# A decoder trunk on one core: the gated convolution's input projection as block products in seven multiplications, and pairs of products taken in turns

## The chip, the cores and the metric

The kernel runs on one core of a Trainium2 chip. The core has a matrix engine (TensorE, PE in the rows; its weight loads are PEld), a vector engine (VectorE, DVE), a scalar engine (ScalarE, ACT), a general engine (GpSimd, POOL), and a queue engine for transfers (SyncE, SP). The metric is the time of one execution on the device in microseconds; the kernel before takes 2549.22 us, the median of 2549.22, 2549.35 and 2545.19.

## What is computed

A trunk of two layers over 1024 tokens of 1024 features, in fp32. Each layer is a mixer, a cross-attention into 256 memory tokens, and an MLP with squared ReLU, each with an RMS norm ahead and a residual added. The mixer of layer 0 is differential attention beside pooling; that of layer 1 is the gated convolution, which the change touches most:

```python
def odd_mixer(h, w_in, conv_w, w_out):
    S = h.shape[1]
    proj = h @ w_in                       # 1024 -> 3 * 1024
    b_gate = proj[..., :CONV_DIM]
    c_gate = proj[..., CONV_DIM:2 * CONV_DIM]
    z = c_gate * proj[..., 2 * CONV_DIM:]
    zp = jnp.pad(z, ((0, 0), (CONV_WIDTH - 1, 0), (0, 0)))
    y = zp[:, 0:S] * conv_w[0]
    for tap in range(1, CONV_WIDTH):
        y = y + zp[:, tap:tap + S] * conv_w[tap]
    return (b_gate * y) @ w_out

for l in range(DEPTH):
    h = h + mixer(rms_norm(h, norm_mix_g[l]))
    h = h + cross_attention(rms_norm(h, norm_xattn_g[l]), mem_n, xattn_wq[l], xattn_wkv[l], xattn_wo[l])
    h = h + sq_relu_mlp(rms_norm(h, norm_mlp_g[l]), mlp_w1[l], mlp_w2[l])
return rms_norm(h, final_norm_g)
```

## The kernel before

**Layout and precision.** Activations lie transposed: 128 features on the partitions, 1024 tokens along a row, eight tiles for 1024 features. A product in fp32 is made of two rounded parts per operand: `cut` writes the high part with a copy on ACT (L72) and the low part with a subtraction on DVE (L73; L75 and L76 where a gain is multiplied in). Three matmuls, high by high, high by low and low by high, make one product of a 128x128 weight tile and 512 tokens. A plain product of one output tile (`gemm`, matmuls on L201) so takes 8 x 3 x 2 = 48 matmuls of 128x512.

**Block products.** `split_gemm` (L277) makes two output tiles at once, in seven steps of 12 matmuls, 84 in all, in place of 96: the weights of the pair and the operand are taken as 2x2 blocks, and four combinations of each ("groups" 0 to 3, the last of half size) are multiplied in seven products. The operand is a `Split` (its groups made by `combine`, L259 to L262), the weights' combinations are made in `w_cut` by four additions on DVE (L149 to L153) and four cuts. The partial sums stand in three PSUM banks (`_x` and the two halves of `_yz`); after each step they are copied out by ACT or added by DVE. With `first` the first four steps are ordered so that parts that come late are used last. A set of `hooks` says what else is issued ahead of which step. Block products serve the queries (`c0q`, `c1q`: four pairs each), MLP up (`m0a`, `m1a`: 16 pairs, evacuated on L1038 and L1042) and MLP down (`m0b`, `m1b`: four chunks `c` of the hidden features by four pairs `p`, added into the residual on L1112). The groups of MLP down's operand are written to DRAM in MLP up and fetched again (`m0f`, L73 rows `m0A_g_k`). The last product of all uses another order of steps, `TAIL`.

**The convolution.** For each of eight tiles j three plain products, `cv{j}c`, `cv{j}x`, `cv{j}b`; the first two are multiplied by the norm's row factors `rbc` and by each other, run through the three taps, and multiplied by the third. MLP down of layer 0 hands over its result as eight cut tiles (L75, L76). The product with conv's output weights (`cvo`) is the `residual`, plain.

**The norm.** Squares are summed on DVE (`acc`), turned by PE (`_n`), reduced on DVE (`_ms`), raised to -1/2 on POOL (`_rcol`), and spread by PE to rows (`_b`), from which `rbc` is read. `stage1` ends with POOL, `stage2` starts with `_b`.

**Order.** The weights come in one list, `order`; SP loads them into four buffers `wr`, and `w_next` hands over a cut and makes the one after it, with two buffers each for `wh` and `wl`. A scheduler of the program's own sets the order of instructions on each engine from the order of the code, its costs and priorities; PE, ACT and DVE then run strictly in that order. 44 slots of 128x1024 hold everything else.

Of the kernel before, what the change touches and what calls it, by code (L numbers as in the profile page):

```python
# [40 lines left out]
def hybrid_trunk(ctx: ExitStack, tc: tile.TileContext, xT, memT, vecs, lams, rel, onehot, negrow, invcnt,  # L41
# [76 lines left out]
    def w_cut():  # L118
        u, g = state["unit"], state["group"]
        if u >= len(order):  # L120
            return
        shape = list(order[u][0])
# [705 lines left out]
    def residual(act, g_col, name, split=False):  # L828
# [55 lines left out]
    def cross(l, X, nrm, g_next, name):  # L884
# [20 lines left out]
        def query(p, hooks):  # L905
# [89 lines left out]
        for p, hooks in enumerate((merged(X.late, {5: [nrm.stage1]}), {1: [divide]}, {},  # L995
# [22 lines left out]
    def mlp(l, X, nrm, g_next, name):  # L1018
# [259 lines left out]
```

## Time and profile before

| | us |
|---|---|
| runs | 2549.22, 2549.35, 2545.19 |
| profiled execution | 2544.53, span 2542.8 |
| PE busy | 2498.8 (98%) |
| DVE busy | 1763.8 (69%) |
| ACT busy | 1073.4 (42%) |
| POOL busy | 25.7 (1%) |

The page is of the profiled execution, whose own time goes with its span. A row of the chain of waits gives the start, the length and the work; a row of PE's waits the engine and tile waited for, the total, the number and the longest; a row of the timeline the start, the length and the instruction, with the idle time before it and what ended it. Rows of the windows give the busy time of PE, PEld, DVE, ACT and POOL in a stretch, then the granted clock, and the share and rate of the transfers. Matmuls overlap in their records: the distance between starts is their pace.

### The profile page before, as it was taken

The page shows a single profiled execution, that of the slowest core. Times are in us where ns is not written, and L with a number is a line of the kernel's source. Part 1 is how long each engine was busy: PE and PEld are TensorE (multiplying, and loading weights), DVE is VectorE, ACT ScalarE, POOL GpSimd, SP SyncE. Part 2 cuts the span into 40 slices and gives each one's busy share as a digit, 9 for nine tenths or more (in the row PEclk, how much of TensorE's full clock was granted, in tenths as well). Part 3 has the DMA queues.
Part 4 walks back from the last instruction along what each step waited for, and adds up shares of the span by engine and source line. Part 5 has one row for each costly group of instructions (what it writes and reads, how often), then busy time and mean ns, then how long its engine had stood idle before and what let it go on. Part 6 is the DMA issues. An engine that isn't in the chain of part 4 may idle for free.

```text
span 2542.8 us, 29713 instructions
## 1 busy us (share of the span) xinstructions
PE 2498.8 (98%) x11522; PEld 2048.1 (81%) x11522; DVE 1763.8 (69%) x2339; ACT 1073.4 (42%) x1513; POOL 25.7 (1%) x24
## 2 busy tenths in 40 slices
PE   9999999999999999999999999999999999999997
PEld 6777778888878888788888888888887888778886
DVE  7777764766677777888784433576667777888876
ACT  5455664445443334443341111344544333434432
POOL 0000000000000000000000000000000000000001
PEclk9999999999999999999999999999999999999998
DMA  5111255221424346877641111422133444777752
GB/s 175 34 34 42 75 169 204 100 83 42 141 88 171 139 145 239 293 270 261 243 154 59 50 50 46 145 75 92 58 117 116 159 160 153 269 266 259 281 207 92
DMA packets 108429, 365.88 MB, mean 144 GB/s; under 512 B 12416, under 2 KB 14848, under 8 KB 108288
## 3 DMA queue, kind: packets, MB, share of 16 engines
q1 hardware_dynamic: 74880, 252.82, 29.5%
q10 hardware_dynamic: 33408, 111.16, 11.4%
q8 instruction: 91, 1.49, 0.2%
q14 instruction: 50, 0.41, 0.0%
HBM read 249.91 MB, written 114.03 MB: 143 GB/s over the span
## 4 chain that ended last, share of the span: by engine, by line
PE 89%; DVE 6%; ACT 2%; DMA 2%; issue 1%; POOL 0%; SPq 0%; ACTq 0%; DVEq 0%; POOLq 0%
PE m0a_x L277 7%; PE m1a_x L277 7%; PE m1b_x L277 7%; PE m0b_x L277 6%; PE m1a_yz L277 5%; PE m0a_yz L277 5%; PE m1b_yz L277 5%; PE m0b_yz L277 4%; PE cvo L201 3%; PE X L201 3%; PE c1o L201 3%; PE c0o L201 3%; PE kv_ps L742 3%; PE qkv L201 2%; PE c1q_x L277 2%; PE c0q_x L277 2%
## 5 line engine op out<-in xcount | busy, mean ns | idle before, releaser
L72 ACT ACTIVATE wh<-wr 128x1024 fp32r<-128x1024 f32 (+1 forms) x318 | 305.6, 961 | 777.7 <-PE m1b_yz L277 137.5
L73 DVE TENSOR_TENSOR wl<-wr,wh 128x1024 fp32r<-128x1024 f32 (+1 forms) x318 | 350.3, 1101 | 135.1 <-ACT wh L72 130.3
L72 ACT ACTIVATE wh<-wt 128x1024 fp32r<-128x1024 f32 x72 | 76.0, 1055 | 60.0 <-PE m0b_x L277 16.5
L73 DVE TENSOR_TENSOR wl<-wt,wh 128x1024 fp32r<-128x1024 f32 x72 | 87.8, 1219 | 0.9 <-ACT wh L72 0.9
L201 PE MATMUL X<-Y,wh 128*128 128x512 f32 x256 | 69.8, 389 | 0.0
L581 ACT ACTIVATE s_p<-s,s_negm 128x128 f32<-128x128 f32 (+7 forms) x64 | 47.3, 739 | 33.6 <-DVE s_negm L580 30.3
L201 PEld LDWEIGHTS X<-Y,wh 128*128 128x128 f32 x256 | 48.1, 188 | 10.0
L149 DVE TENSOR_TENSOR wt<-wr 128x512 f32<-128x512 f32 x71 | 48.8, 687 | 6.8 <-DMA wr<-in_w_dram 3.1
L150 DVE TENSOR_TENSOR wt<-wr,wt 128x512 f32<-128x512 f32 x71 | 48.9, 689 | 1.3
L152 DVE TENSOR_TENSOR wr<-wr,wr 128x512 f32<-128x512 f32 x71 | 48.7, 687 | 1.0
L153 DVE TENSOR_TENSOR wr<-wr,wt 128x512 f32<-128x512 f32 x71 | 48.6, 684 | 0.0
L1028 ACT ACTIVATE m0a_r<-m0a_r 128x1024 f32<-128x1024 f32 x32 | 33.9, 1061 | 32.0 <-DVE m0a_r L1027 31.9
L1028 ACT ACTIVATE m1a_r<-m1a_r 128x1024 f32<-128x1024 f32 x32 | 33.9, 1060 | 32.0 <-DVE m1a_r L1027 31.8
L580 DVE TENSOR_REDUCE s_negm<-s 128x1 f32<-128x128 f32 (+7 forms) x64 | 46.6, 750 | 0.2
L1042 DVE TENSOR_TENSOR m0a_r<-m0a_r,m0a_yz 128x512 f32<-128x512 f32 x32 | 21.9, 685 | 31.3 <-PE m0a_yz L277 31.1
L1042 DVE TENSOR_TENSOR m1a_r<-m1a_r,m1a_yz 128x512 f32<-128x512 f32 x32 | 21.9, 685 | 31.3 <-PE m1a_yz L277 31.1
L1038 ACT ACTIVATE m0a_r<-m0a_x 128x512 f32<-128x512 f32 x32 | 19.1, 598 | 55.7 <-PE m0a_x L277 53.8
L1038 ACT ACTIVATE m1a_r<-m1a_x 128x512 f32<-128x512 f32 x32 | 19.1, 598 | 55.5 <-PE m1a_x L277 53.9
L201 PE MATMUL X<-Y,wl 128*128 128x512 f32 x128 | 40.7, 389 | 0.0
L277 PE MATMUL m0b_x<-m0A,wh 128*128 128x512 f32 x128 | 39.5, 390 | 0.7 <-DVE m0b0h L1112 0.7
L277 PE MATMUL m0a_x<-c0o_x,wh 128*128 128x512 f32 x128 | 39.6, 390 | 0.0
L277 PE MATMUL m1a_x<-c1o_x,wh 128*128 128x512 f32 x128 | 39.5, 390 | 0.0
(2681 smaller groups left out, 7678.9 us busy)
## 6 DMA issues: line engine op xcount, KB each, us to landing
wr<-in_w_dram SPq DMA_DIRECT2D x128, 512.0 KB, 4.0
m0f<-m0a_d SPq DMA_DIRECT2D x48, 512.0 KB, 6.4
m1f<-m1a_d SPq DMA_DIRECT2D x48, 512.0 KB, 6.0
wr<-in_wkv_dram SPq DMA_DIRECT2D x32, 512.0 KB, 3.5
m0a_d<-m0a_r ACTq DMA_DIRECT2D x32, 512.0 KB, 2.8
m1a_d<-m1a_r ACTq DMA_DIRECT2D x32, 512.0 KB, 2.9
wr<-in_conv_in_dram SPq DMA_DIRECT2D x24, 512.0 KB, 3.6
wr<-in_wq_dram SPq DMA_DIRECT2D x16, 512.0 KB, 3.6
```

What stands on the lines that cost most here:

```text
L72: nc.scalar.activation(hi, src, AF.Copy)
L73: nc.vector.tensor_sub(lo, src, f32(hi))
L149: nc.vector.tensor_add(t[:, 4:], b[:, :4], b[:, 4:])
L150: nc.vector.tensor_sub(t[:, :4], a[:, :4], t[:, 4:])
L152: nc.vector.tensor_sub(a[:, :4], b[:, :4], a[:, :4])
L153: nc.vector.tensor_add(a[:, 4:], a[:, 4:], t[:, :4])
L201: nc.tensor.matmul(ps, wt[:, k, :], act.part(k, i, h), start=(k == 0 and wt is hi and i == 0), stop=(k == ks - 1 and wt is lo))
L277: nc.tensor.matmul(banks[b], w[a][:, 4 * (i % 2) + j, :], act.part(g, s, j, c), start=(new and j == 0 and n == 0), stop=(j == nk - 1 and n ...
L580: nc.vector.tensor_reduce(s["negm"][:, m : m + 1], ps[:, :L], axis=AX.X, op=ALU.max, negate=True)
L581: nc.scalar.activation(s["pr"][m][:, :L], ps[:, :L], AF.Exp, bias=s["negm"][:, m : m + 1], accum_out=s["den"][:, m : m + 1])
L742: nc.tensor.matmul(ps[mt], mem["x"][i][k // 4][:, k % 4, mt * P : (mt + 1) * P], w[j][:, kk, :], start=(k == 0 and n == 0), stop=(k == KT ...
L1028: nc.scalar.activation(t, t, AF.Square)
```

## The change

1. The convolution's 24 plain products become 12 block products (`product`, over pairs of tiles). The gating works on copies in SBUF: c times x times the squared row factors, taps, row factors, b. The input weights' layout is permuted for it.
2. The end of MLP down of layer 0 makes a `Split` for it: `scale` on ACT, `sums` (the combinations on DVE), group 0 cut at once. Groups 1 to 3 of the first two pairs go to DRAM (`put`, six transfers on ACT's queue) and come back (`get`, six on SP's); they are cut (`made`) at the end of MLP down and in the first convolution products (`nx.late`). The last product of MLP down has the order `TAIL` in both layers now. The squares for the norm of the last tiles, and `stage1`, move to the second convolution product.
3. `in_turns`: the first two pairs at the convolution, the queries and both MLP products run in turns: two steps of the one, two of the other, two and two again, then four and four. Steps 0 and 1 need combination 0 of the weights only, so the list `seq` sets the order of weight cuts accordingly, and the second pair's additional buffer is a slot. What was hung on the first two products (`divide`, `ready`, `late`) is spread anew.
4. Before the convolution's output, the first two products are interleaved: six of their eight operand tiles for both, then the last two.

```diff
+        turns.add(len(order))
         order += [(FLAT, w1[l, 2 * p], w1[l, 2 * p + 1]) for p in range(4 * KT // 2)]
+        turns.add(len(order))
         order += [(FLAT, w2[l, c, 2 * p], w2[l, c, 2 * p + 1]) for c in range(4) for p in range(KT // 2)]
...
+        if u in turns:
+            seq += [(u, 0), (u + 1, 0), (u, 1), (u + 1, 1), (u, 2), (u, 3), (u + 1, 2), (u + 1, 3)]
+            u += 2
...
+    def in_turns(one, two):
+
+        for it, n in ((one, 2), (two, 2), (one, 2), (two, 2), (one, 4), (two, 4)):
+            for _ in range(n):
+                next(it, None)
...
+        two = []
+        if late:
+            two = [(w_next(), psg(f"{name}_0")), (cuts[state["used"]], psg(f"{name}_1"))]
+            state["used"] += 1
+            for ks in (range(KT - 2), range(KT - 2, KT)):
+                for w, ps in two:
+                    for k in ks:
+                        steps([(h, ps[:, half(h)]) for h in range(2)], w, act, k)
...
+        def scale(t, p, h):
+            raws_x[p, 2 * h] = slot(f"{name}x{p}_r{h}")
+            for i in range(2):
+                nc.scalar.activation(raws_x[p, 2 * h][:, i * H : (i + 1) * H], t[i][:, half(h)], AF.Copy,
+                                     scale=col(g_next + 2 * p + i))
...
+        def put(p):
+            for g in range(1, 4):
+                xd[p, g] = dp.tile([P, S if g < 3 else H], F32, name=f"{name}x{p}_d{g}")
+                nc.scalar.dma_start(xd[p, g], raws_x.pop((p, g)))
+
+        def get(g):
+            for p in range(2):
+                x = slot(f"{name}xf{g}_{p}")
+                raws_x[p, g] = x if g < 3 else x[:, :H]
+                nc.sync.dma_start(raws_x[p, g], xd[p, g])
...
+                if tail and not fin:
+                    todo.append({2: [lambda: get(1)], 4: [lambda: made(1, 0)],
+                                 5: [lambda: scale(t, p, 0), lambda: first_group(p), lambda: made(1, 1)],
+                                 6: [lambda: made(1, 2), lambda: get(2)]})
...
+                    nx.late = ({2: [lambda: get(3)], 3: [lambda: made(2, 0)], 4: [lambda: made(2, 3)],
+                                5: [lambda: made(3, 0, 1)], 6: [lambda: made(3, 2, 3)]},
+                               {2: [lambda: made(2, 1)], 3: [lambda: made(2, 2)],
+                                4: [lambda: nn.add(kept[2][0]), lambda: nn.add(kept[2][1]), keep],
+                                5: [lambda t=t: nn.add(t[0])], 6: [lambda t=t: nn.add(t[1]), nn.stage1]})
...
-        for j in range(KT):
-            nm = f"{name}{j}"
-            psc = gemm(X, f"{nm}c", hooks.pop(0) if hooks else None)
-            cg, z = slot(f"{nm}_cg"), slot(f"{nm}_z")
...
+        for j in range(KT // 2):
+            nm, last = f"{name}{j}", j == KT // 2 - 1
             if j == 0:
-                nc.vector.tensor_mul(cg, psc, nrm.rbc)
...
+                c, one = product(f"{nm}c", X.late[0], first=True, run=False)
+                x, two = product(f"{nm}x", X.late[1], run=False)
+                in_turns(one, two)
+            else:
+                c = product(f"{nm}c", merged(before, {4: [parts(0)]} if last else {}))
+                x = product(f"{nm}x", {1: [parts(1)], 3: [parts(2)]} if last else {})
```

Three places in the order of DVE's instructions. First, the start of MLP down in layer 0 (`m0b`; `wl_g` is the low part of weight combination g, `m0A_g_k` the operand's group g, tile k; L1112 before and L1189 now add a step's sum into the residual). Before:

```order
L1112 TENSOR_TENSOR m0b0h_8287<-m0b0h_8287,m0b_0_yz 128x512
L73 TENSOR_TENSOR wl_1_8470<-wt_8429,wh_1_8469 128x1024
L73 TENSOR_TENSOR wl_2_8512<-wr_0_8219,wh_2_8511 128x1024
L73 TENSOR_TENSOR m0A_1_3l<-m0f_1_3_8339,m0A_1_3h 128x1024
L149 TENSOR_TENSOR wt_8603<-wr_1_8379 128x512
L1027 SCALAR_TENSOR_TENSOR m0a_r_8291<-m0a_r_8291,c0o_rbc 128x1024
L1112 TENSOR_TENSOR m0b0h_8287<-m0b0h_8287,m0b_0_x 128x512
L73 TENSOR_TENSOR m0A_2_0l<-m0f_2_0_8381,m0A_2_0h 128x1024
L1112 TENSOR_TENSOR m0b0h_8289<-m0b0h_8289,m0b_0_yz 128x512
L73 TENSOR_TENSOR m0A_2_1l<-m0f_2_1_8383,m0A_2_1h 128x1024
```

And now:

```order
L1189 TENSOR_TENSOR m0b0h_8287<-m0b0h_8287,m0b_0_yz 128x512
L73 TENSOR_TENSOR wl_0_8474<-wr_0_8377,wh_0_8473 128x1024
L73 TENSOR_TENSOR wl_1_8515<-wt_8429,wh_1_8514 128x1024
L1062 SCALAR_TENSOR_TENSOR m0a_r_8291<-m0a_r_8291,c0o_rbc 128x1024
L162 TENSOR_TENSOR wt_8475<-wr_1_8379 128x512
L163 TENSOR_TENSOR wt_8475<-wr_0_8377,wt_8475 128x512
L73 TENSOR_TENSOR m0A_1_3l<-m0f_1_3_8339,m0A_1_3h 128x1024
L1189 TENSOR_TENSOR m0b0h_8467<-m0b0h_8467,m0b_1_x 128x512
L165 TENSOR_TENSOR wr_0_8377<-wr_1_8379,wr_0_8377 128x512
L1189 TENSOR_TENSOR m0b0h_8467<-m0b0h_8467,m0b_1_yz 128x512
```

The second pair's combination 0 (`wl_0_8474`) now stands ahead of the first pair's combination 1, and the cuts of operand group 2 come after the second pair's first two steps (`m0b_1`).

Second, the end of MLP down and the start of the convolution. Before (`m0b_x6l`, `m0b_x7l` are the last two tiles handed over, `wl_0_10821` the first convolution weights):

```order
L1112 TENSOR_TENSOR m0b3h_10594<-m0b3h_10594,m0b_3_x 128x512
L1112 TENSOR_TENSOR m0b3h_10592<-m0b3h_10592,m0b_3_yz 128x512
L73 TENSOR_TENSOR wl_0_10821<-wr_0_10650,wh_0_10820 128x1024
L76 SCALAR_TENSOR_TENSOR m0b_x6l<-m0b3h_10592,vec,m0b_x6h 128x1024
L1112 TENSOR_TENSOR m0b3h_10594<-m0b3h_10594,m0b_3_x 128x512
L324 TENSOR_TENSOR m0b_acc<-m0b_acc,m0b_sq 128x1024
L76 SCALAR_TENSOR_TENSOR m0b_x7l<-m0b3h_10594,vec,m0b_x7h 128x1024
```

And now (`m0x_k` are the operand's groups for the convolution, `m0xf` what came back from DRAM, `wl_0_10872` the first pair's and `wl_0_10921` the second pair's combination 0):

```order
L73 TENSOR_TENSOR m0x_3l<-m0x_r_10846,m0x_3h 128x1024
L1189 TENSOR_TENSOR m0b3h_10697<-m0b3h_10697,m0b_3_yz 128x512
L1189 TENSOR_TENSOR m0b3h_10695<-m0b3h_10695,m0b_3_yz 128x512
L73 TENSOR_TENSOR m0x_1l<-m0xf_1_10778,m0x_1h 128x1024
L1189 TENSOR_TENSOR m0b3h_10695<-m0b3h_10695,m0b_3_x 128x512
L73 TENSOR_TENSOR wl_0_10872<-wr_0_10665,wh_0_10871 128x1024
L73 TENSOR_TENSOR m0x_2l<-m0x_t_10797,m0x_2h 128x1024
L165 TENSOR_TENSOR wr_0_10665<-wr_1_10667,wr_0_10665 128x512
L166 TENSOR_TENSOR wr_0_10665<-wr_0_10665,wt_10873 128x512
L270 TENSOR_TENSOR m0x_t_10904<-m0x_r_10901,m0x_r_10846 128x512
L73 TENSOR_TENSOR wl_0_10921<-wr_0_10820,wh_0_10920 128x1024
```

The first convolution weights, which stood ahead of the last addition, stand behind it now, and more cuts and combinations stand on both sides of them.

Third, the norm's reductions in the convolution. Before:

```order
L73 TENSOR_TENSOR wl_0_10858<-wr_0_10652,wh_0_10857 128x1024
L333 TENSOR_REDUCE m0b_ms<-m0b_n_10894 128x4
L333 TENSOR_REDUCE m0b_ms<-m0b_n_10900 128x4
L335 TENSOR_SCALAR m0b_ms<-m0b_ms 128x8
L73 TENSOR_TENSOR wl_0_10929<-wr_0_10786,wh_0_10928 128x1024
```

And now:

```order
L73 TENSOR_TENSOR wl_0_11178<-wr_0_11067,wh_0_11177 128x1024
L355 TENSOR_REDUCE m0b_ms<-m0b_n_11189 128x4
L165 TENSOR_TENSOR wr_0_11067<-wr_1_11069,wr_0_11067 128x512
L166 TENSOR_TENSOR wr_0_11067<-wr_0_11067,wt_11179 128x512
L355 TENSOR_REDUCE m0b_ms<-m0b_n_11195 128x4
L73 TENSOR_TENSOR wl_1_11221<-wt_11179,wh_1_11220 128x1024
L357 TENSOR_SCALAR m0b_ms<-m0b_ms 128x8
```

The three steps of the norm, which followed each other, now have three weight operations between them. On PE the order holds 10104 matmuls of 128x512 where it held 10248.

More of the change, by code (lines that the diff above doesn't have):

```diff
@@ L81, in hybrid_trunk @@
     FLAT = (P, KT, P)
-    order = [(FLAT, w_in[8])]
+    order, tails, turns = [(FLAT, w_in[8])], set(), set()
     for h in range(1, 4):
@@ L118, in w_cut @@
     def w_cut():
-        u, g = state["unit"], state["group"]
-        if u >= len(order):
+        if state["cut"] >= len(seq):
             return
+        u, g = seq[state["cut"]]
         shape = list(order[u][0])
@@ L161, in w_cut @@
         cuts.append((hi, lo))
-        state["group"] += 1
+        state["cut"] += 1
         if done:
             state["held"] -= min(len(raw), 2)
-            state["unit"] += 1
-            state["group"] = 0
             w_load()
     def w_next():
-        while len(cuts) < state["used"] + 2 and state["unit"] < len(order):
+        while len(cuts) < state["used"] + 2 and state["cut"] < len(seq):
             w_cut()
@@ L928, in evac @@
                         cut(*Q.t[2 * p], r[0])
-            split_gemm(X, f"{name}q{p}", evac, hooks, first=(p == 0))
+            steps = split_steps(X, f"{name}q{p}", evac, hooks, first=(p == 0))
+            if not run:
+                return steps
+            for _ in steps:
+                pass
         def divide():
@@ L994, in cross @@
         n = len(units)
[L995 removed]
+        in_turns(query(0, merged(X.late, {5: [nrm.stage1]}), False), query(1, {5: [divide]}, False))
+        for p, hooks in ((2, {}), (3,
                                    {1: [lambda: kv_load(0)], 2: [lambda: kv_cut(0)],
@@ L1042, in evac @@
                     nc.vector.tensor_add(d, d, ps)
-            split_gemm(X, nm, evac, hooks, first=(p == 0))
+            steps = split_steps(X, nm, evac, hooks, first=(p == 0))
+            if run:
+                for _ in steps:
+                    pass
             x = []
@@ L1088, in mlp @@
         rest, ahead = merged(X.late, {5: [nrm.stage1], 6: [nrm.stage2]}), []
-        for p in range(2 * KT):
+        r0, one = up(0, rest, False)
+        rest, two = up(1, {4: r0[1], 5: r0[2], 6: r0[3]}, False)
+        in_turns(one, two)
+        rest = merged(rest, {4: r0[5]})
+        for p in range(2, 2 * KT):
             if p == 2 * KT - 1:
@@ L1176, in conv_mixer, with product, evac @@
-        return residual(Y, g_next, f"{name}o", split=True)
+        Y, ys = Halves(), {}
+        sq = {}
+        def product(nm, hooks, first=False, run=True):
+            r = [slot(f"{nm}_r{n}") for n in range(2)]
+            def evac(n, h, ps, new):
+                d = r[n][:, half(h)]
+                if new:
+                    nc.scalar.activation(d, ps, AF.Copy)
+                else:
+                    nc.vector.tensor_add(d, d, ps)
+            steps = split_steps(X, nm, evac, hooks, first=first)
+            if not run:
+                return r, steps
+            for _ in steps:
+                pass
+            return r
@@ L1178, in hybrid_trunk @@
+        for n in range(2):
+            times(n)()
+            parts(KT - 2 + n)()
+        return residual(Y, g_next, f"{name}o", split=True, late=True)
     X, nrm = cross(0, X, nrm, G_MLP[0], "c0")
@@ L1247, in _layout @@
     g["pool_w"] = a["pool_w"][0].transpose(1, 0, 2)
-    g["conv_in"] = tiles(a["conv_w_in"][0])
     g["conv_out"] = tiles(a["conv_w_out"][0])
@@ L1253, in _layout @@
     halves = [0, 2, 4, 6, 1, 3, 5, 7]
+    g["conv_in"] = tiles(a["conv_w_in"][0])[..., halves, :]
     g["wq"] = tiles(a["xattn_wq"])[..., halves, :]
```

159 lines of the change are left out of this document (110 added, 49 removed).

## The prediction

> **What bounds the kernel now.** I read the page's first part, then the chain of waits and what PE waits for, then windows and timelines of the places that the change touches.
>
> ```profile
> PE 2498.8 (98%) x11522; PEld 2048.1 (81%) x11522; DVE 1763.8 (69%) x2339; ACT 1073.4 (42%) x1513; POOL 25.7 (1%) x24
> core 0: 2542.8 us, clock 0.997
> ...
> 1052.03 2.72 PE m0b_x L277 x12
> ...
> 1356.31 10.88 PE cv0b L201 x48
> ...
> 1584.79 10.88 PE cv7b L201 x48
> 1595.67 81.60 PE cvo L201 x360
> ```
>
> PE is the bound: 98% busy at a granted clock of 0.997. The chain (start, length, work, count) gives its pace: 10.88/48 = 0.2267 us for a 128x512 matmul in the plain products of the convolution, 2.72/12 = 0.2267 in the block products. So a matmul less is 0.2267 us less, wherever it stood, as long as the other engines follow. The 24 convolution products pass without a stall: from the first row for cv0b to the end of the last are 22 x 10.88 = 239.4 us, and 1595.67 - 1356.31 = 239.36. All that PE loses by waiting at the places of this change is in the waits (total us, times, longest):
>
> ```profile
> PE m1b_b L345 <- POOL m1b_rcol L336: 4.3, 2, 3.7
> PE m0a_x L277 <- DVE wl L73: 1.3, 1, 1.3
> PE c0q_x L277 <- ACT c0q_r L920: 1.0, 1, 1.0
> PE m0a_x L277 <- ACT m0a_r L1038: 1.0, 1, 1.0
> PE m0b_yz L277 <- DVE m0b0h L1112: 0.9, 1, 0.9
> PE m0b_x L277 <- DVE m0b0h L1112: 0.7, 1, 0.7
> PE m0b_x L277 <- DVE m0A_3l L73: 0.6, 1, 0.6
> PE m0b_x L277 <- DVE m0A_0l L73: 0.6, 1, 0.6
> PE m0b_x L277 <- DVE wl L73: 0.4, 1, 0.4
> PE c0o_b L345 <- POOL c0o_rcol L336: 0.2, 1, 0.2
> ...
> 1028.14 0.39 PE L277 MATMUL m0b_x<-m0A_0l,wh 128*128 128x512 f32 x1
> 1029.43 0.50 PE L277 MATMUL m0b_yz<-m0A_0h,wh 128*128 128x512 f32 x1 [0.91 <-DVE m0b0h L1112]
> ```
>
> Layer 1's rows (c1, m1) read the same. The last two rows price a wait: start to start 1.29 us in place of 0.227, so 1.06 is lost where the view says 0.91. I add 0.17 to each wait of the list.
>
> **Part 1: conv_in in seven multiplications.** 24 products of 48 matmuls become 12 of 84: PE issues 1152 - 1008 = 144 fewer. 144 x 0.2267 = **-32.6 us**, if DVE keeps up, since it gets the new work: per group of three products (c, x, b for two tiles) 12 weight combinations, 9 cuts of 128x1024 and 3 of half the size, 9 additions out of PSUM, and the gating. Its prices:
>
> ```profile
> L73 DVE TENSOR_TENSOR wl<-wt,wh 128x1024 fp32r<-128x1024 f32 x72 | 87.8, 1219 | 0.9 <-ACT wh L72 0.9
> L149 DVE TENSOR_TENSOR wt<-wr 128x512 f32<-128x512 f32 x71 | 48.8, 687 | 6.8 <-DMA wr<-in_w_dram 3.1
> ...
> 1320.09 0.68 DVE L1112 TENSOR_TENSOR m0b3h<-m0b3h,m0b_yz 128x512 f32<-128x512 f32 x1
> 1320.68 1.22 DVE L73 TENSOR_TENSOR wl<-wr,wh 128x1024 fp32r<-128x1024 f32 x1
> 1321.90 0.69 DVE L1112 TENSOR_TENSOR m0b3h<-m0b3h,m0b_x 128x512 f32<-128x512 f32 x1
> 1322.50 1.22 DVE L324 TENSOR_TENSOR m0b_acc<-m0b_acc,m0b_sq 128x1024 f32<-128x1024 f32 x1
> ...
> 727.30:1011.30 284.00, 282.50 (x1247) 231.82 (x1246) 214.16 (x272) 114.35 (x138) 1.64 (x1) 1.00 0.46 165
> 1049.00:1330.00 281.00, 280.93 (x1239) 232.24 (x1238) 224.91 (x281) 109.32 (x119) 0.00 (x0) 1.00 0.68 241
> 1333.00:1596.00 263.00, 263.00 (x1170) 218.02 (x1169) 109.54 (x102) 46.56 (x51) 1.64 (x1) 1.00 0.18 58
> ```
>
> Queued back to back, a 128x512 operation costs 0.6 us (1320.09 to 1320.68) and a 128x1024 one 1.2. Weights per product: 4 x 0.6 + 3 x 1.2 + 0.6 = 6.6; three are 19.8. Additions 9 x 0.6 = 5.4. Gating and taps, some 12 full operations x 1.2 = 14.4. Together 39.6 us in 3 x 84 x 0.2267 = 57.1 us, 69%. The windows (length, then busy time of PE, PEld, DVE, ACT, POOL) show block products at full PE pace with more: 214.2 of 284 (75%) in MLP up, 224.9 of 281 (80%) in MLP down; convolution now has 109.5 of 263. So nothing is taken off the 32.6 inside the stage. ACT (114 of 284 in MLP up) is far from the limit.
>
> In the Trainium skill, "TensorE: Matmul & The Clock Gate", section "Wait — 56ns, not 53.3ns?", a warm 512-column matmul starts 215.7 ns after the one before; by that the term would be 144 x 0.2157 = 31.1. The row says 226.7, and goes ahead.
>
> **Part 2: pairs in turns.** Where the second matmul group needed a bank that is still being emptied, or a part not yet cut, PE now works on the other pair.
>
> Queries: the 1.0 <- ACT c0q_r goes in both layers: 2 x 1.17 = **-2.4**. Bounds 0 (another wait takes its place) and -2.4.
>
> MLP up: the 1.0 <- ACT m0a_r goes too, 1.17. But before c0o_b multiplies the norm's factors, only 12 matmuls (2.7 us) are left as cover. Before, half of the transposes and their reduction (c0o_n) were done 24 matmuls earlier; now both halves stand in front of these 12, one more reduction (0.6) lies in the way, and the wait for c0o_rcol, 0.2, grows to 0.8. Net -0.6 a layer, **-1.2**; bounds 0 and -2.4. The 1.3 <- DVE wl at the end of MLP up stays: DVE's order there is as before.
>
> MLP down: the five waits sum to 0.9 + 0.7 + 0.6 + 0.6 + 0.4 = 3.2, with 5 x 0.17 some 4.05 us. DVE is full there:
>
> ```profile
> 1022.00:1050.00 28.00, 24.80 (x103) 18.56 (x102) 27.67 (x34) 15.36 (x18) 0.00 (x0) 1.00 0.72 261
> ```
>
> 27.67 of 28 us. In turns the first 24 + 24 matmuls need only group 0 of the operand, but the second pair's weights too, so wl_0 of the second pair moves ahead of the cuts of groups 2 and 3. Walking DVE's new order at 0.6 and 1.2, I find PE waiting 0.35 for the first pair's second combination and 0.5 for the second pair's first: 0.85 left. 4.05 - 0.85 = 3.2 a layer, **-6.5** in both. What DVE owes then is late next, in the third product, whose window has 20% to spare. Bounds: 0 (DVE is full, so its sum sets the time whatever PE's order) and -8.1.
>
> **Part 3: the way from MLP down into the convolution.** Before, no wait stands there. Now the last product's end must be scaled, combined into four groups, and cut; three of the groups of the first two pairs come back from DRAM; and conv's first weights stand behind that on DVE.
>
> ```profile
> 1330.06 0.69 DVE L1112 TENSOR_TENSOR m0b3h<-m0b3h,m0b_yz 128x512 f32<-128x512 f32 x1 [2.03 <-PE m0b_yz L277]
> 1330.92 1.23 DVE L73 TENSOR_TENSOR wl<-wr,wh 128x1024 fp32r<-128x1024 f32 x1 [0.18 <-ACT wh L72]
> ...
> 1330.79 1.14 ACT L75 ACTIVATE m0b_x6h<-m0b3h,vec 128x1024 fp32r<-128x1024 f32 x1
> ...
> 1339.38 1.03 PE L332 MATMUL m0b_n<-ident,m0b_acc 128*128 128x128 f32 x8
> 1341.59 1.64 POOL L336 TENSOR_TENSOR m0b_rcol<-m0b_ms,mhalf 128x8 f32<-128x8 f32 x1 [611.00 <-DVE m0b_ms L335]
> ...
> m0f<-m0a_d SPq DMA_DIRECT2D x48, 512.0 KB, 6.4
> m0a_d<-m0a_r ACTq DMA_DIRECT2D x32, 512.0 KB, 2.8
> ```
>
> DVE idled 2.03 us there; in the new order its rows from the last product's first addition up to its last are 16 of 128x512 and 5 of 128x1024, 16 x 0.6 + 5 x 1.2 = 15.6 us, in six steps of 12 matmuls, 16.3 us. Whatever waits here holds up all of conv behind it on PE, and DVE's additions after that. The walk from T0, PE's last matmul of MLP down: the cut of m0x_3l waits for ACT (scale 0.6, copy 1.05) until T0 - 2.7; it, two additions, the cut of m0x_1l and the last addition end at T0 + 1.45; wl_0 of cv0c follows, to T0 + 2.65. PE asks for it after four matmuls, T0 + 0.9: about 1.85 lost. Behind wl_0 in DVE's queue are four combinations and the cut for group 1's last part, on which PE waits 0.65 more; a later weight cut costs 0.15. Last, the norm: before, the factors were there 3.85 us after the transposes began (1339.38 to 1341.59 + 1.64) and nothing waited, since 24 matmuls lay between. Now 23 do (5.2 us), so the factors are wanted 6.0 after the start with the transposes' 0.8; but the two reductions and the step behind them share DVE's queue with four weight operations (2 x 0.6 + 2 x 1.2 = 3.6): 3.85 + 3.6 = 7.45, and the first of these waits for ACT's copy of the same weights (1.05; I take half): 1.9 lost. Sum 1.85 + 0.65 + 0.15 + 1.9, **+4.5 us**. Bounds: 0, as in the trace of before, and 9.6, if all eleven DVE rows from wl_0 to group 1's last cut (5 x 1.2 + 6 x 0.6) pass with PE idle. I take the walk.
>
> The way back from DRAM (2.8 out, 6.4 in) has over a product's 19 us; the loads stand on SP between weight loads for conv, which wait for their buffers longer than that; the six stores add six issues to ACT's queue, which is under half full. No cost. The convolution's end, with its last gated parts ahead of the first conv_out products (two now interleaved): **+0.65**, bounds 0 and 2.7 (12 matmuls).
>
> **Sum.** -32.6 - 2.4 - 1.2 - 6.5 + 4.5 + 0.65 = -37.55. On the profiled execution's 2544.5 us (span 2542.8) this is 2507; its time is 4.7 below the median of 2549.2, which would give 2511.6. Two of three runs lie at the median, one and the profiled one lie 4 below. I forecast **2509 us**. With every term at its lower bound the sum is -32.6 - 2.4 - 2.4 - 8.1 = -45.5, with every one at its upper -32.6 + 9.6 + 2.7 = -20.3: 2501 and 2526.
>
> **Rivals.**
>
> *DVE, not PE, sets the end of MLP down (chance 0.20).* For: 15.6 of 16.3 us is hardly a margin; one late scale on ACT or one late load adds to T0 directly, and what is left over pushes into cv0c, whose own weights are DVE work. Against: the window of MLP down shows 80% with full pace. If the last product and the first pair of conv lose 3 to 5 more each, and the turns at MLP down bring nothing (+6.5) or what I counted: 6 to 16.5 above the forecast, 2515 to 2526.
>
> By the Trainium skill ("TensorE: Matmul & The Clock Gate", "What's actually happening") PE falls to half its clock after an idle window of about 3.4 us. The trace bears it out at the kernel's end:
>
> ```profile
> 2530.00:2540.00 10.00, 1.12 (x4) 0.72 (x4) 6.17 (x11) 0.60 (x1) 3.51 (x3) 0.50 0.95 349
> ```
>
> After the 3.7 us wait for m1b_rcol the granted clock reads 0.50. My largest new wait is 1.9, below that; in this rival one could pass it and cost 1.7 to 3.4 us more. That stays inside its times.
>
> *No new wait at the two ways (0.10).* The scheduler set the order, and 1.85 hangs on one cut: 5.15 less than the forecast, 2504.
>
> *DVE bounds the whole convolution: slower (0.03).* Place: the three products of a group. It decides from the point where DVE takes over 57.1 us per group; for no gain at all it must take 57.1 + 37.6/4 = 66.5, against 39.6 counted. Even if each of the 9 additions and the 12 weight combinations waits 0.9 for its partner, it is 39.6 + 18.9 = 58.5. Price then: 4 x (58.5 - 57.1) = 6 us, and to be slower, 38. 2552 us.
>
> *The change doesn't do what it says (0.02).* The count of matmuls in the order is 144 lower, so this could only be a slower pace: 32.6/1008 = 0.032 us per matmul. The two equal rows speak against it: 2549.
>
> **How the numbers follow.** Forecast 0.65 (2504 to 2515: the walk's terms right within a half), DVE at the end of MLP down 0.20, no new wait 0.10, slower 0.03, unchanged 0.02. The range of 2500 to 2521 holds the forecast, the better rival and half of the worse: 0.85, less what I don't foresee. A difference under 0.2% (5 us) is what this measurement can't tell from none: faster 0.95, same 0.02, slower 0.03.
>
> **What would show it.** Right: 12 convolution products of 19.04 us each at a distance of 0.2267 per matmul; no row c0q_x <- ACT c0q_r and m0a_x <- ACT m0a_r; MLP down beginning with under 1 us of waits; one new wait of 1 to 3 us by cv0c for DVE wl and one by m0b_b for POOL m0b_rcol. Wrong: DVE over 90% in the conv window, PE waiting for wl in each product of it, waits of over 10 us in sum between MLP down and cv0b, or a clock under 0.98 in that window.

## The result, and the profile after

The changed kernel takes 2515.01 us (median of 2511.44, 2513.59, 2516.43 and 2519.23) where the kernel before takes 2547.20: the ratio is 0.9875, with a 95% interval of 0.9854 to 0.9895. That is 32 us less; 2509 was forecast, with a range of 2500 to 2521. The profiled execution took 2511.44 us, with a span of 2509.7 against 2542.8, 33.1 us less; the forecast's sum was 37.6 less.

The page and the view of the cores of the changed kernel:

```profile
PE 2466.0 (98%) x11378; PEld 2021.3 (81%) x11378; DVE 1842.6 (73%) x2465; ACT 1133.6 (45%) x1610; POOL 29.8 (1%) x24
...
core 0: 2509.7 us, clock 0.997
```

PE is still the bound, with 144 matmuls (11522 to 11378) and 32.8 us of busy time less; DVE has 79 us more and still idles for a quarter of the span. What PE waits for at the places of the change (of MLP up and down, layer 0's rows):

```profile
PE m0b_b L367 <- POOL m0b_rcol L358: 3.6, 1, 3.6
PE cv0c_x L298 <- DVE wl L73: 1.6, 1, 1.6
PE c1o_b L367 <- POOL c1o_rcol L358: 1.4, 1, 1.4
PE c0o_b L367 <- POOL c0o_rcol L358: 1.4, 1, 1.4
PE m0a_x L298 <- DVE wl L73: 1.3, 1, 1.3
PE c1q_x L298 <- DVE wl L73: 0.5, 1, 0.5
PE c0q_x L298 <- DVE wl L73: 0.5, 1, 0.5
PE m0b_x L298 <- DVE wl L73: 0.4, 1, 0.4
```

The waits that the turns were to remove are gone (m0a_r, c0q_r, m0b0h, m0A_3l, m0A_0l). Two that were foreseen stand at the way into the convolution, cv0c for wl at the size foreseen (1.6, 1.77 by the distance between starts, against 1.85), m0b_b for the norm's factors at twice the size foreseen (3.6, 3.80 by distance, against 1.9).

To see where the time went, I took the distances between the first matmuls of neighbouring stages in both traces. The names are those of the stage's products; "cv0" runs from the convolution's first matmul to the first with its output weights.

| stage | before | changed | difference | forecast |
|---|---|---|---|---|
| up to the queries | 484.4 | 484.6 | +0.2 | 0 |
| queries (c0q, c1q) | 129.6, 129.6 | 128.7, 128.7 | -1.8 | -2.4 |
| attention's output (c0o, c1o) | 91.9, 91.9 | 91.9, 91.9 | 0 | 0 |
| MLP up (m0a, m1a) | 316.5, 316.5 | 316.3, 316.3 | -0.4 | -1.2 |
| MLP down (m0b, m1b and the end) | 310.2, 327.6 | 306.5, 324.9 | -6.4 | -6.5 |
| convolution in (cv0) | 262.9 | 238.0 | -24.9 | -32.6 + 4.5 = -28.1 |
| convolution out (cvo) | 81.6 | 81.9 | +0.3 | +0.65 |

3.2 of the 4.5 us that are missing against the forecast are missing in the convolution. Windows of the changed kernel, with the columns length, busy PE, PEld, DVE, ACT, POOL, granted clock, share and rate of transfers:

```profile
1329.00:1557.50 228.50, 223.26 (x984) 184.02 (x984) 170.65 (x198) 92.78 (x124) 4.28 (x1) 0.99 0.18 55
...
1371.00:1376.00 5.00, 1.74 (x8) 1.12 (x6) 4.51 (x6) 0.60 (x1) 3.96 (x1) 1.00 0.00 0
1376.00:1379.00 3.00, 2.63 (x11) 2.44 (x12) 0.00 (x0) 1.19 (x2) 0.32 (x1) 0.50 0.00 0
...
1385.00:1555.00 170.00, 170.00 (x751) 140.37 (x750) 122.37 (x141) 62.53 (x83) 0.00 (x0) 1.00 0.18 56
```

From 1385 on PE is busy for 170.00 of 170 us and does 751 matmuls, one every 0.2264 us, with DVE at 72%: DVE does not limit the block products there. DVE's 170.65 us over the stage are 75%; 69% was counted. All of the convolution's loss lies ahead of 1380, and the largest piece is in one place. PE there:

```profile
1372.35 0.39 PE L298 MATMUL cv0b_yz<-m0x_0h,wl 128*128 128x512 f32 x1
1376.37 1.97 PE L367 MATMUL m0b_b<-ident,m0b_rcol 128*128 128x128 f32 x8 [3.63 <-POOL m0b_rcol L358]
1377.99 0.78 PE L298 MATMUL cv0b_yz<-m0x_1h,wh 128*128 128x512 f32 x1
1378.57 0.63 PE L298 MATMUL cv0b_yz<-m0x_1l,wh 128*128 128x512 f32 x1
1378.99 0.58 PE L298 MATMUL cv0b_yz<-m0x_1h,wl 128*128 128x512 f32 x1
1379.41 0.40 PE L298 MATMUL cv0b_yz<-m0x_2h,wh 128*128 128x512 f32 x1
1379.64 0.39 PE L298 MATMUL cv0b_yz<-m0x_2l,wh 128*128 128x512 f32 x1
```

and DVE and POOL at the same time:

```profile
1371.80 0.16 DVE L357 TENSOR_SCALAR m0b_ms<-m0b_ms 128x8 f32<-128x8 f32 x1
1371.87 2.35 DVE L1298 TENSOR_TENSOR cv0c_r<-cv0c_r,cv0x_r 128x1024 f32<-128x1024 f32 x2
1374.14 0.68 DVE L162 TENSOR_TENSOR wt<-wr 128x512 f32<-128x512 f32 x1
1374.86 0.69 DVE L163 TENSOR_TENSOR wt<-wr,wt 128x512 f32<-128x512 f32 x1
...
1372.04 4.28 POOL L358 TENSOR_TENSOR m0b_rcol<-m0b_ms,mhalf 128x8 f32<-128x8 f32 x1 [631.80 <-DVE m0b_ms L357]
```

POOL's step, on the same 8 values per row, took 1.64 us here before and takes 4.28 now. PE stands still for 3.6 us, and then runs at a granted clock of 0.50: matmuls start 0.58 and 0.42 apart, and at 0.23 again from 1379.41 on. Two theories were open: that POOL is held up by what DVE does beside it, and that the half clock comes from the pause. Both could be tested.

### The profile page after: what moved, and what is told of

Its sections match the earlier page's. It is cut to its first block, busy times and chain, and to the rows that moved or that the text cites. A ratio compares the mean times of both kernels' runs of the same rounds, so it can differ in the third digit from the quotient of the medians.

```text
span 2509.7 us, 29710 instructions
## 1 busy us (share of the span) xinstructions
PE 2466.0 (98%) x11378; PEld 2021.3 (81%) x11378; DVE 1842.6 (73%) x2465; ACT 1133.6 (45%) x1610; POOL 29.8 (1%) x24
## 4 chain that ended last, share of the span: by engine, by line
PE 88%; DVE 7%; ACT 3%; issue 1%; DMA 1%; POOL 1%; SPq 0%; DVEq 0%; ACTq 0%; POOLq 0%
PE m0a_x L298 7%; PE m1a_x L298 7%; PE m0b_x L298 7%; PE m1b_x L298 6%; PE m0a_yz L298 5%; PE m1a_yz L298 5%; PE m0b_yz L298 5%; PE m1b_yz L298 5%; PE cvo L212 3%; PE X L212 3%; PE c0o L212 3%; PE c1o L212 3%; PE kv_ps L764 3%; PE qkv L212 2%; PE u L212 2%; PE c1q_x L298 2%
## 5 line engine op out<-in xcount | busy, mean ns | idle before, releaser
L73 DVE TENSOR_TENSOR wl<-wr,wh 128x1024 fp32r<-128x1024 f32 (+1 forms) x330 | 358.4, 1086 | 163.7 <-ACT wh L72 159.8
L72 ACT ACTIVATE wh<-wt 128x1024 fp32r<-128x1024 f32 x84 | 88.8, 1057 | 85.9 <-PE m1b_x L298 14.4
L73 DVE TENSOR_TENSOR wl<-wt,wh 128x1024 fp32r<-128x1024 f32 x84 | 102.3, 1218 | 0.7 <-ACT wh L72 0.7
L212 PE MATMUL cvo<-cvg,wh 128*128 128x512 f32 x256 | 69.8, 389 | 0.0
L162 DVE TENSOR_TENSOR wt<-wr 128x512 f32<-128x512 f32 x82 | 56.3, 686 | 6.8 <-DMA wr<-in_w_dram 3.1
L163 DVE TENSOR_TENSOR wt<-wr,wt 128x512 f32<-128x512 f32 x82 | 56.5, 688 | 1.5
L165 DVE TENSOR_TENSOR wr<-wr,wr 128x512 f32<-128x512 f32 x82 | 56.3, 686 | 1.0
L212 PEld LDWEIGHTS cvo<-cvg,wh 128*128 128x128 f32 x256 | 48.0, 188 | 10.4 <-ACT wh L72 0.4
L166 DVE TENSOR_TENSOR wr<-wr,wt 128x512 f32<-128x512 f32 x82 | 56.1, 684 | 0.0
L212 PE MATMUL cvo<-cvg,wl 128*128 128x512 f32 x128 | 40.6, 389 | 0.0
```

The source lines that it names most:

```text
L72: nc.scalar.activation(hi, src, AF.Copy)
L73: nc.vector.tensor_sub(lo, src, f32(hi))
L162: nc.vector.tensor_add(t[:, 4:], b[:, :4], b[:, 4:])
L163: nc.vector.tensor_sub(t[:, :4], a[:, :4], t[:, 4:])
L165: nc.vector.tensor_sub(a[:, :4], b[:, :4], a[:, :4])
L166: nc.vector.tensor_add(a[:, 4:], a[:, 4:], t[:, :4])
```

## The experiments

Each is the changed kernel with one edit, unless said otherwise. Spans are those of the profiled executions.

**The convolution's norm later.** The factors are spread two steps later.

```diff
-                hooks = {1: [nrm.stage2, squared], 2: [gate(0)], 3: [taps(0)], 4: [gate(1)], 5: [taps(1)],
-                         6: [scaled(0), scaled(1)]}
+                hooks = {3: [nrm.stage2, squared], 4: [gate(0)], 5: [taps(0), gate(1)], 6: [taps(1), scaled(0), scaled(1)]}
```

> The norm's spreading (m0b_b) in the convolution's third product comes two steps (24 matmuls, 5.4 us) later, and what needs it with it. Theory: the wait of 3.6 us for POOL m0b_rcol and the half clock behind it (matmul distances of 0.42 to 0.58 us instead of 0.227 for 3 us, some 2.0 us lost) are one loss with one cause; both go, the span falls from 2509.7 by 3.8 + 2.0 = 5.8 to about 2504, and POOL's step still takes about 4.3 us. Rival: the factors are late for everybody, and the wait turns up at the third product's end or in the next product (PE waiting for DVE or ACT), so that the span falls by under 2 us. Second rival: the slow matmuls have nothing to do with the wait; then only 3.8 go.

2506.92 us, ratio to before 0.9844 (0.9829 to 0.9859), span 2505.2. The interval just touches the changed kernel's (0.9854 to 0.9895), so the stage has to tell: the convolution's goes from 238.0 to 233.0 us. In its trace:

```profile
1372.80 4.28 POOL L358 TENSOR_TENSOR m0b_rcol<-m0b_ms,mhalf 128x8 f32<-128x8 f32 x1 [632.78 <-DVE m0b_ms L357]
...
1376.00:1379.00 3.00, 3.00 (x20) 2.56 (x18) 2.25 (x3) 1.17 (x3) 1.08 (x1) 1.00 0.13 11
...
1378.19 1.04 PE L367 MATMUL m0b_b<-ident,m0b_rcol 128*128 128x128 f32 x8
```

POOL is as slow as before, nobody waits for it, the clock stays at 1.00, and the eight transposes take 1.04 instead of 1.97 us. The loss is one: both parts go together, and the rival that the slow matmuls have nothing to do with the wait falls. It is 5.0 us in the stage, where 5.8 was expected. The span fell by 4.5, since MLP down waited 0.9 us longer for weights in this execution.

**DVE beside POOL: two inputs or one.** Only for the first pair, the product c times x is left out, and in the one kernel two reductions stand in its place.

```diff
-                    nc.vector.tensor_mul(c[n], c[n], x[n])
+                    if j > 0:
+                        nc.vector.tensor_mul(c[n], c[n], x[n])
+                    else:
+                        m = small.tile([P, 1], F32, tag="red", name=f"red{n}")
+                        nc.vector.tensor_reduce(m, x[n], axis=AX.X, op=ALU.add)
```

> Two DVE multiplications of 128x1024 (c times x in the first pair; two inputs in SBUF each), which run while POOL raises the norm's 8 values per row to -1/2, are replaced by two reductions of 128x1024 with one input in SBUF and about the same length. The product c times x of the first pair is so left out. Theory: POOL's step is slowed from 1.64 to 4.28 us by DVE instructions with two inputs in SBUF; with reductions it takes 1.7 to 2.2, PE's wait for m0b_rcol falls from 3.6 to 1.0 to 1.6 us, the half clock behind it goes, and the span is about 2505. Rival: any busy DVE slows POOL; the step stays at 4 us or more and the wait at 3.6. Second rival: POOL's step is as long as it is whatever DVE does; the same.

> The same two multiplications are left out with nothing in their place, so DVE's next work beside POOL's step are two additions of 128x512 (two inputs in SBUF, 1.2 us) instead of 2.3 us of multiplications and then the additions. Theory: POOL's step takes between the two, 2.2 to 3.0 us, PE's wait 1.5 to 2.4, no half clock, span 2504 to 2507. Rival (POOL doesn't depend on DVE): 4.3 and 3.6 as before.

With the reductions (a single execution, 2511.75 us, span 2510.0):

```profile
1375.48 0.16 DVE L357 TENSOR_SCALAR m0b_ms<-m0b_ms 128x8 f32<-128x8 f32 x1
1375.55 2.33 DVE L1302 TENSOR_REDUCE red<-cv0x_r 128x1 f32<-128x1024 f32 x2
...
1375.72 1.64 POOL L358 TENSOR_TENSOR m0b_rcol<-m0b_ms,mhalf 128x8 f32<-128x8 f32 x1 [632.15 <-DVE m0b_ms L357]
...
PE m0b_b L367 <- POOL m0b_rcol L358: 1.0, 1, 1.0
```

With nothing in their place (a single execution, 2509.58 us, span 2507.8):

```profile
1373.05 0.69 DVE L162 TENSOR_TENSOR wt<-wr 128x512 f32<-128x512 f32 x1
1373.78 0.69 DVE L163 TENSOR_TENSOR wt<-wr,wt 128x512 f32<-128x512 f32 x1
...
1373.18 2.06 POOL L358 TENSOR_TENSOR m0b_rcol<-m0b_ms,mhalf 128x8 f32<-128x8 f32 x1 [632.78 <-DVE m0b_ms L357]
...
1375.29 1.09 PE L367 MATMUL m0b_b<-ident,m0b_rcol 128*128 128x128 f32 x8 [1.40 <-POOL m0b_rcol L358]
```

DVE is busy for the whole of POOL's step in the first kernel, with 2.33 us of reductions where 2.35 us of multiplications stood, and POOL takes 1.64 us, as beside an idle DVE. So it isn't work on DVE as such that slows POOL, and POOL isn't slow by itself at this place. With nothing in their place it took 2.06, where 2.2 to 3.0 was expected, and the rows show why. The first addition was under way when POOL's step began and had 0.56 us left (1373.05 + 0.69 - 1373.18); POOL lost 0.42. The second began 0.04 us after the first had ended and cost POOL nothing. In the changed kernel the two multiplications and the addition on L162 follow each other without a gap, and 2.78 us of them are left when POOL begins (1374.14 + 0.68 - 1372.04); POOL lost 2.64. L163, again behind a gap of 0.04, cost nothing. So POOL is held up until the run of two-input instructions that it met comes to its first gap, and then takes its 1.64 us, less 0.14.

Two steps in the profile of before say the same:

```profile
206.09 0.43 DVE L73 TENSOR_TENSOR at_0l<-tp,at_0h 128x256 fp32r<-128x256 f32 x1
206.23 1.64 POOL L336 TENSOR_TENSOR sub_rcol<-sub_ms,mhalf 128x8 f32<-128x8 f32 x1 [70.75 <-DVE sub_ms L335]
...
278.75 1.21 DVE L73 TENSOR_TENSOR wl<-wr,wh 128x1024 fp32r<-128x1024 f32 x1
278.91 2.54 POOL L336 TENSOR_TENSOR sub_rcol<-sub_ms,mhalf 128x8 f32<-128x8 f32 x1 [71.04 <-DVE sub_ms L335]
```

The second met a cut with 1.05 us left and lost 0.90. The first met a cut of the same kind whose operand `tp` lies in PSUM, with 0.29 left, and lost nothing, where 0.15 would be due. So a TENSOR_TENSOR holds POOL up only if both of its operands are in SBUF. The eleven traces hold 110 POOL steps of this size; 59 of them met such a run of instructions, and all 110 follow this rule within 0.02 us.

The Trainium skill ("SBUF — State Buffer", section "SBUF: two separate sides") says that DVE instructions with two SBUF inputs and GpSimd take one pair of ports in turns, and that the one that comes second is fully blocked. For POOL coming second the rows agree: 2.78 us left, 2.64 lost. For DVE coming second they don't: L163 began 2.82 us into POOL's step of 4.28 and took its usual 0.69.

The convolution's stage took 233.9 us with the reductions, 4.1 less than in the changed kernel. By distance, PE's wait for the factors fell from 3.80 to 1.15, which is 2.65 of it; the half clock is the rest, about 1.4. The span of that execution, 2510.0, where about 2505 was expected, did not fall: its queries began 3.4 us later than the changed kernel's, most of it from another stretch at half clock, between 299 and 308 us, told of below. So these single spans say less than the stage.

**Turns at MLP down undone.** The pairs run one after the other in both layers, with the former hooks.

```diff
-        turns.add(len(order))
         order += [(FLAT, w2[l, c, 2 * p], w2[l, c, 2 * p + 1]) for c in range(4) for p in range(KT // 2)]
...
-                if (c, p) == (0, 0):
-                    one = steps
-                elif (c, p) == (0, 1):
-                    in_turns(one, steps)
-                else:
-                    for _ in steps:
-                        pass
+                for _ in steps:
+                    pass
```

> Only the turns at MLP down are undone, in both layers: the first two pairs run one after the other, with the hooks that they had before. Theory: the five waits at each start of MLP down come back (4.05 us a layer) for the 0.96 and 1.3 us that stand there now; the span rises by 3.1 + 2.8 = 5.9 to about 2515.6, and the rest is unchanged. Rival: DVE, full in that stretch, sets the time whatever PE's order; then the turns bring nothing and the span stays within 1 us of 2509.7.

2519.98 us, ratio 0.9889 (0.9872 to 0.9905). The old waits are back, in both layers:

```profile
PE m0b_yz L297 <- DVE m0b0h L1185: 0.9, 1, 0.9
PE m1b_yz L297 <- DVE m1b0h L1185: 0.9, 1, 0.9
PE m0b_x L297 <- DVE m0b0h L1185: 0.7, 1, 0.7
PE m1b_x L297 <- DVE m1A_3l L73: 0.6, 1, 0.6
PE m0b_x L297 <- DVE m0A_3l L73: 0.6, 1, 0.6
```

MLP down grows from 306.5 to 310.2 us and from 324.9 to 328.9: 3.7 and 4.0 where 3.1 and 2.8 were expected. So the rival that DVE, full in that stretch, would give the turns nothing falls. It falls by the stages and the waits: the medians differ by 5.0 us, but their intervals overlap. The span, 2522.1, is 12.4 higher; 3.7 of that lie ahead of the queries, most of it in the stretch at half clock.

**Turns alone.** The convolution and the end of MLP down of layer 0 as before the change.

```diff
-                order += [(FLAT, conv_in[i * KT + 2 * j], conv_in[i * KT + 2 * j + 1]) for i in (1, 2, 0)]
+                order += [(FLAT, conv_in[i * KT + j]) for i in (1, 2, 0)]
...
-                c, one = product(f"{nm}c", X.late[0], first=True, run=False)
-                x, two = product(f"{nm}x", X.late[1], run=False)
-                in_turns(one, two)
+            psc = gemm(X, f"{nm}c", hooks.pop(0) if hooks else None)
+            psx = gemm(X, f"{nm}x", hooks.pop(0) if hooks else None)
```

> Only the turns, at the queries and both MLP products; the convolution's products stay plain, with 48 matmuls each, and MLP down of layer 0 hands over cut tiles as before. Theory: PE gains 2 x (1.17 - 0.66) at the queries, nothing at MLP up, 3.1 + 2.8 at MLP down: 6.9 us, a span of about 2536; no new wait between MLP down and the convolution, and POOL's m0b_rcol at 1.64 us. So the other 26 us of the change come from the convolution: -32.6 and 7 back at its start. Rival: the turns at MLP down bring what they do only because of other parts; then the span is over 2540.

2534.98 us, ratio 0.9955 (0.9940 to 0.9970), span 2533.1: 9.7 less than before, where 6.9 was expected from the waits of the changed kernel and 10.1 stood in the forecast. The stages give -0.9 at each of the queries, -0.1 and -0.2 at MLP up, -4.0 and -3.5 at MLP down; the convolution has its old 262.9. POOL and PE there:

```profile
1336.55 1.64 POOL L357 TENSOR_TENSOR m0b_rcol<-m0b_ms,mhalf 128x8 f32<-128x8 f32 x1 [596.34 <-DVE m0b_ms L356]
...
PE c0o_b L366 <- POOL c0o_rcol L357: 1.5, 1, 1.5
PE c1o_b L366 <- POOL c1o_rcol L357: 1.5, 1, 1.5
```

The other 23.4 us (2533.1 - 2509.7) came with the convolution's block products: 25.0 in its own stage, less some 1.6 in the others. POOL's m0b_rcol is at its 1.64 us where the gating of block products isn't beside it.

**The convolution's first pair in sequence.** No turns there; the cuts of groups 2 and 3 stand earlier.

```diff
...
-                c, one = product(f"{nm}c", X.late[0], first=True, run=False)
-                x, two = product(f"{nm}x", X.late[1], run=False)
-                in_turns(one, two)
+                c = product(f"{nm}c", X.late[0], first=True)
+                x = product(f"{nm}x", X.late[1])
```

> The convolution's first two block products run one after the other instead of in turns; the operand's groups 2 and 3 are so wanted 24 to 36 matmuls (5 to 8 us) earlier, and are cut earlier. All else is as changed. Theory: DVE, without a gap from the end of MLP down on, is what cv0c waits for; new waits for the cuts of groups 1 to 3 of 4 to 9 us in sum between cv0c and cv0x, span 2514 to 2519. Rival: the products wait for the weights only, and the order of the pairs makes under 1 us.

A single execution: 2526.03 us, span 2524.3, the convolution's stage 247.2 instead of 238.0.

```profile
1342.56 0.50 PE L297 MATMUL cv0c_x<-m0x_0h,wh 128*128 128x512 f32 x1 [2.40 <-ACT cv0c_r L1267]
1342.90 0.40 PE L297 MATMUL cv0c_x<-m0x_0l,wh 128*128 128x512 f32 x1
1344.72 0.80 PE L297 MATMUL cv0c_yz<-m0x_0h,wh 128*128 128x512 f32 x1 [1.43 <-DVE cv0c_r L1269]
1345.32 0.63 PE L297 MATMUL cv0c_yz<-m0x_0l,wh 128*128 128x512 f32 x1
...
1344.00:1346.00 2.00, 1.28 (x3) 1.09 (x4) 2.00 (x4) 2.00 (x3) 0.00 (x0) 0.50 0.51 199
```

There are new waits of 2.4 and 1.4 us for the emptying of cv0c's banks, 4.2 by distance, and a half clock behind them; the wait for the norm's factors grows from 3.6 to 4.0, and the half clock behind that one lasts longer. The new waits are at the low end of what was expected (4 to 9), and the releaser is another: PE doesn't wait for the operand's cuts themselves, but ACT and DVE come to the banks only behind such cuts and cuts of weights. The rival, that the order makes under 1 us, falls. The span is 5 us above the expected range: it is 14.6 longer than the changed kernel's, 9.2 in this stage and 4.5 ahead of the queries, where this execution has a stretch at half clock near 300 us. The turns hide the waits for the banks.

**The output's first two products in order.** The interleaving is undone.

```diff
-        return residual(Y, g_next, f"{name}o", split=True, late=True)
+        return residual(Y, g_next, f"{name}o", split=True)
```

> Only the interleaving of the first two products with the convolution's output weights is undone: the first runs through all eight tiles, then the second. Theory: the last two tiles, gated at the end of the convolution's last product, are wanted after 36 matmuls (8.2 us) instead of 72 (16.3 us); their chain is two multiplications, two additions out of PSUM and four copies and subtractions on ACT and DVE, some 6 to 8 us, so PE waits 0 to 3 us and the stage of conv's output grows from 81.9 to 82 to 85 us. Rival: the tiles come much later than that (DVE behind), and PE waits over 3 us; then interleaving hides more than I counted.

A single execution, 2513.5 us. The stage is 81.9 us long, as with the interleaving, and PE has no wait for a gated tile in either. Nothing here shows that part 4 of the change is worth anything.

**Both norms later.** With the convolution's norm as above, and in MLP up:

```diff
-        rest, ahead = merged(X.late, {5: [nrm.stage1], 6: [nrm.stage2]}), []
+        rest, ahead = merged(X.late, {5: [nrm.stage1]}), []
...
-        rest, two = up(1, {4: r0[1], 5: r0[2], 6: r0[3]}, False)
+        rest, two = up(1, {4: [nrm.stage2] + r0[1], 5: r0[2], 6: r0[3]}, False)
```

> As the one with the convolution's norm two steps later, and in MLP up of both layers the spreading of the norm's factors (c0o_b, c1o_b) stands 12 matmuls later, in the second pair. Theory: the wait of 1.38 us for POOL c0o_rcol (1.54 by distance) goes in both layers and nothing takes its place: 3.1 us under the kernel with the convolution's norm alone, so a span of 2502 and PE's waits without c0o_b and c1o_b. Rival: the squares on DVE, which need the factors, come late for the next combinations, and PE waits for DVE instead; then it is the same as with the convolution's norm alone.

2502.75 us (2502.39 to 2503.55), ratio 0.9829 (0.9814 to 0.9844), span 2500.6. MLP up falls from 316.3 us by 1.9 in each layer, where 1.54 was expected, the convolution is at 232.9, and at the places of the change no wait for POOL is left. Of what was run this is the shortest by its median; its interval doesn't touch the changed kernel's.

**And the first weights ahead.** On top of that, `w_cut` for the convolution's first combination runs with a higher priority of the scheduler.

```diff
+        if (u, g) in hasten and not state.get("hst"):
+            state["hst"] = True
+            with tc.high_priority():
+                w_cut()
+            state["hst"] = False
+            return
```

> As the one with both norms later, and the first convolution weights' combination 0 is cut with a higher priority, which in the order puts wl_0 ahead of the last addition of MLP down and of the cut m0x_1l, behind which it stood. Theory: the 1.6 us of PE's wait for DVE wl at cv0c goes, but PE wants m0x_1l two matmuls later, which is now 2.4 us later on DVE: a wait of about 1 us for m0x_1l instead, net gain 0.5 to 1.0 us. Rival: DVE's queue simply shifts, and the gain is 1.6; or it costs, since the last addition frees a bank later.

2504.71 us, ratio 0.9840 (0.9821 to 0.9859), span 2500.3: no difference from the one above that can be told. The wait for wl (1.6) is gone, and there is a new one, which is neither of those expected:

```profile
PE cv0c_yz L305 <- DVE cv0c_r L1277: 0.8, 1, 0.8
```

PE waits 0.8 us for the emptying of a bank, some 10 us later; the stage gains 0.5 (232.4 from 232.9), the low end of the 0.5 to 1.0 expected.

## Why the prediction was right, and where it was off

The forecast was right in its direction and mechanism, and the time lies in its range, 6 us above the value. By its own steps:

- **Part 1, 144 matmuls less at 0.2267.** Right. PE's pace is unchanged (0.2264 us for a matmul over 170 us), and DVE keeps up in all that follows the norm. The rival that DVE bounds the whole convolution is refuted by that window, the rival of a slower pace too.
- **Part 2, queries, -2.4.** -1.8. The wait for c0q_r went; 0.5 us (0.66 by distance) for a weight cut in c0q came, which I hadn't counted.
- **Part 2, MLP up, -1.2.** -0.4. The step "the wait for c0o_rcol grows to 0.8" was mis-sized: 1.4. POOL's step took 2.06 us there instead of 1.64, which is 0.4 of the difference.
- **Part 2, MLP down, -6.5.** -6.4; 7.7 where its turns are undone, 7.5 where the turns stand alone. Walking DVE's order gave this well: 0.97 us of waits are left at each start by distance, for 0.85. That the sum fits within 0.1 is in part luck, as the layers gave 3.7 and 2.7 where 3.2 was forecast for each.
- **Part 3, +4.5.** The step that failed. cv0c's wait was right (1.77 for 1.85); 0.65 and 0.15 did not come; but the norm's wait, 1.9, measured 3.8, and some 1.5 of half clock followed it. DVE was even quicker than I had walked: the transposes begin at 1366.48 and DVE's last step ends at 1371.96, 5.5 later, where 7.9 - 1.64 = 6.3 was counted. The mis-sized term is POOL's 1.64 us, taken from a row where DVE was idle: 4.28. Beside the multiplications that the change itself puts there, it is another number. The profile of before already held a POOL step of the same size at 2.54 us, beside a cut on DVE (278.91, shown above), and the walk didn't use it. The text's own sign, a wait of 1 to 3 us by m0b_b, was missed for this reason.
- **The convolution's end, +0.65.** +0.3 in the stage; nothing to be had there.
- **The clock.** The text let the half clock come in only with the rival that DVE sets the end of MLP down. It came without that rival, behind the 3.6 us wait for POOL.

The five points add up: queries 0.6, MLP up 0.8, MLP down 0.1, the convolution 3.2 and its output -0.35 are 4.35 of the 4.45 us between -37.55 and -33.1. The rest of the 6 us, some 1.5, is the level and not the mechanism: the forecast lay between the profiled execution's and the median's, and the changed kernel's runs spread from 2511 to 2519.

Two small slips in the working change nothing: the row that prices a wait gives 0.15 us above the view where 0.17 is added (0.16 and 0.17 were measured since), and 3.2 a layer at MLP down is 6.4, not 6.5.

The rival *DVE sets the end of MLP down* did not come. PE waits for nothing in that stage's last products. DVE came late enough to hold up the convolution's banks where the turns there were taken away and, by 0.8 us, where the first weights were put ahead.

## What to carry to other kernels

A duration is only as good as its neighbours: before a price is taken from a row, look at what the other engines do beside it there, and what they will do beside it in the new order, above all for the few instructions that a whole engine waits for. A chain over a slow engine (here transposes, reduction, POOL, transposes) should be issued early and used late: two hooks moved by one or two steps were worth 9 us by the spans (2509.7 to 2500.6) and by the stages, over a quarter of what the whole change brought; the medians, 2515.0 and 2502.8, differ by 12. And taking two independent products in turns pays where PSUM banks or cuts are late, by 3.5 to 4 us at each start of MLP down, measured apart from the rest, and by 9 at the convolution's start, in a single execution and about half of it at half clock. At MLP up it brought 0.2 us, as the wait for the norm's factors took the place of the wait for a bank until the norm was moved too.

## What the runs showed of the hardware

POOL's TENSOR_TENSOR of 128x8 takes 1.64 us when DVE, as the step begins, is idle, at a reduction, or at an instruction with an operand in PSUM. When it meets a TENSOR_TENSOR of DVE with both operands in SBUF, it is longer by what is left of that instruction and of those that follow without a gap, less 0.14 us: 2.06 us for 0.56 left, 2.54 for 1.05, 4.28 for 2.78. Two-input work on DVE that begins after a gap adds nothing. Nor did a SCALAR_TENSOR_TENSOR of 128x256 with both operands in SBUF that followed a cut without a gap (279.88 in the profile of before); why is open.

The granted clock fell to 0.50 after a pause of 3.6 us, which is what the Trainium skill ("TensorE: Matmul & The Clock Gate", section "What's actually happening") has, with a window of about 3.4 us. It did so too where no single pause was that long: at 1344 us with the convolution's pair in sequence, after 2.4 and 1.4 us with two matmuls in between, and near 300 us in three of the eleven profiled executions (the reductions, the turns at MLP down undone, the convolution's pair in sequence), where PE was busy most of the time. The kernel with the reductions had that stretch, the changed kernel's profiled execution did not:

```profile
299.00:302.00 3.00, 2.91 (x10) 1.68 (x9) 3.00 (x7) 2.56 (x5) 0.00 (x0) 0.69 0.17 25
302.00:305.00 3.00, 3.00 (x11) 2.12 (x10) 1.76 (x3) 0.00 (x0) 0.00 (x0) 0.50 0.41 150
305.00:308.00 3.00, 3.00 (x13) 2.63 (x13) 0.41 (x1) 0.38 (x1) 0.00 (x0) 0.67 0.00 0
```

It cost about 3.0 us: POOL's norm step ahead of the stretch began at 279.57 instead of 279.12 in the changed kernel, the one behind it at 357.40 instead of 353.95. The granted clock also goes with the spread between runs of one kernel: the four runs of the changed kernel have mean clocks of 0.997, 0.996, 0.995 and 0.994 with spans of 2509.7, 2511.6, 2514.3 and 2517.2. What makes that stretch fall in one execution and not in the next was not tried, and stays open.
